# Down projections as seven block products, with block sums made during the gate stages

## The chip, the cores and the metric

The kernel runs on one core of one Trainium2 chip. The metric is the device time of one execution in microseconds; the figure for a kernel is the median of its runs. The time before is 2503.31 us (three runs, 2498.36 to 2503.79).

## The reference

Two decoder layers over 1024 tokens of width 1024, in float32. Layer 0 uses sliding-window attention, layer 1 stick-breaking attention; each attention and each channel mixer is normalised, scaled by the conditioning vector `c`, and added to the residual through a gate. What the change touches is the channel mixer:

```python
D_FF = 2816
def swiglu(h, w_gate, w_up, w_down):
    return (jax.nn.silu(h @ w_gate) * (h @ w_up)) @ w_down
...
    for i in range(DEPTH):
        mod = (cond @ ada_w[i] + ada_b[i])[:, None, :]
        sh1, sc1, g1, sh2, sc2, g2 = jnp.split(mod, 6, axis=-1)
        ...
        h = rmsnorm(x, norm2_g[i]) * (1.0 + sc2) + sh2
        x = x + g2 * swiglu(h, w_gate[i], w_up[i], w_down[i])
```

`c` is (1, 1024), `x` is (1, 1024, 1024), `w_gate` and `w_up` are (2, 1024, 2816), `w_down` is (2, 2816, 1024).

## The kernel before, in words

The program runs through these stages, with their place in the profiled span in microseconds: norm and attention of layer 0 (to about 335), its output projection with the second norm (335 to 452), the gates of layer 0 (452 to 905), down of layer 0 (907 to 1148), attention of layer 1, its output projection, the gates of layer 1 (1850 to 2249), down of layer 1 (2251 to 2493).

Every product is done in three matmuls. An operand is split into a rounded high part and a remainder (ScalarE casts, VectorE subtracts: `split_s` with L629/L630 in the gates, `split_into` with L308/L309 elsewhere), and `mm3` (L108) multiplies high by high, low by high and high by low, each 128x128 by 128x512.

**Gates** (`gates`, L816). 22 feature tiles are taken two at a time, so there are 11 chunks. A chunk splits the 1024 tokens in two halves and its weights in 2x2 blocks, and makes for the gate matrix and for the up matrix seven block products instead of eight (`first_product` with B11, then B21, T2, T3, N4, T1, B22): 14 products of 12 matmuls, 168 in all. The block sums of the weights are made by GpSimd (`block_sums`, L804 to L806, and L812), 8 operations a chunk. Sums of products are read from PSUM by VectorE (L814, L840, L848, L851, L855, L858). Two PSUM banks of tag `z` hold T2, T3 and N4 in turn: the sum u2 (L814) has to be read before T3 may add to the same bank, and u3 (L848) before N4 may. At the end SiLU (ScalarE) and a multiply (L862) make four quarters of the hidden tile, which go to DRAM (`hid`, stores at L841 and L863).

In layer 0 the gates also carry the conditioning products of layer 1. `ada_step` (L262) loads 512 KB tiles into the pool `ad`, which has two buffers, and VectorE multiplies and accumulates them (L268); every eighth such step ends in 8 small matmuls. `grow_make` borrows the same pool once.

**Down** (`down`, L873). The hidden tiles and the rows of `w_down` are loaded again, 44 tiles of 512 KB a layer. The weight tile is multiplied by the gate row g2 (L889), both are split (L308, L309), and 22 x 8 x 2 x 3 = 1056 matmuls a layer run in six rounds of up to four feature tiles. Each bank is added to the accumulator `xacc` by VectorE (`evict`, L906), 96 times a layer. `xacc` is loaded at the start from `xsp` (`load_acc`, L941), and stored by block at the end.

**Order.** Each engine works through its own list in a fixed order, and so does the queue of SyncE that issues nearly all DMAs: an instruction that waits holds back all that stand behind it in its list. The build makes these lists from the program text, its priorities and the reuse of buffers; they aren't the order of the text. `rows(range(4, 8))` in `out_proj` (L671, L672 on GpSimd) belongs to the norm between output projection and gates.

Of the kernel before, what the change touches and what calls it, by code (L numbers as in the profile page):

```python
# [64 lines left out]
def build(tc, x_in, c_in, pos_in, ada_w, ada_b, n1g, n2g, wqkv_a, qn_a, kn_a, sinks, wo_a,  # L65
# [750 lines left out]
    def gates(l, H, p, fp, hid, ada_per, first):  # L816
# [10 lines left out]
        def chunk(c):  # L827
            if c == 0:
                m = first["m"]
            else:  # L830
# [10 lines left out]
            nc.sync.dma_start(hid[2 * c][:, 0:512], g11)  # L841
# [17 lines left out]
            for n, i, j in (("p1", 1, 0), ("u3", 1, 1), ("u2", 0, 1)):  # L859
# [16 lines left out]

    def down(l, rawp, nraw, dn, xacc, hid, row, finish):
        f0 = 0
        for r, n in enumerate(ROUNDS):
            g = r % 2  # L880
            T = []
            for j in range(n):
                f = f0 + j
                t = []
                for e, src in enumerate((hid[f], w_down[l][f * P : (f + 1) * P])):
                    raw = rawp.tile([P, D], F32, tag="raw", name=nm("raw"), bufs=nraw)
                    ld = nc.sync.dma_start(raw, src)
                    if e:
                        nc.vector.tensor_tensor(raw, raw, row, op=ALU.mult)  # L889
                    h = dn.tile([P, D], F32R, tag=f"{'ab'[e]}h{g}{j}", name=nm("dh"), bufs=1)  # L890
                    l_ = dn.tile([P, D], F32R, tag=f"{'ab'[e]}l{g}{j}", name=nm("dl"), bufs=1)
                    t += split_into(h, l_, raw)
                T.append(t)
            f0 += n
            if r == 0:
                with tc.issue_after(ld.ins):
                    load_acc(xacc)

            def one(pb, b, h, j):
                ah, al, bh, bl = T[j]  # L900
                mm3(pb, ah[:, b * P : (b + 1) * P], al[:, b * P : (b + 1) * P],
                    bh[:, h * 512 : (h + 1) * 512], bl[:, h * 512 : (h + 1) * 512], j == 0, j == n - 1)

            def evict(pb, b, h):
                xs = xacc[b][:, h * 512 : (h + 1) * 512]
                nc.vector.tensor_tensor(xs, pb, xs, op=ALU.add)  # L906

            if r == 0:
                pbs = [bank(t) for t in BANKS]
                for j in range(n):  # L910
                    for i in range(8):
                        one(pbs[i], i // 2, i % 2, j)
                for i in range(8):
                    evict(pbs[i], i // 2, i % 2)
            for b in range(4 if r == 0 else 0, NB):
                for h in range(2):
                    pb = bank(BANKS[(2 * b + h) % 8])
                    for j in range(n):
                        one(pb, b, h, j)
                    evict(pb, b, h)  # L920
                if r == len(ROUNDS) - 1:
                    finish(b)

    def mixer(l, W, p, od, x_src, gi, ada_per, rest, row):
# [308 lines left out]
```

## Time and profile before

| | before |
|---|---|
| median of three runs, us | 2503.31 |
| profiled execution, us | 2499.7 |
| its span, us | 2497.6 |
| mean granted clock of TensorE | 0.978 |
| TensorE matmuls, busy us (share of span) | 2355.8 (94%) |
| VectorE, busy us | 1615.5 (65%) |
| ScalarE, busy us | 1034.4 (41%) |
| GpSimd, busy us | 641.1 (26%) |
| moved by DMA, MB | 273.78 |

The span is what the trace covers; 2.1 us of the profiled execution's time lie around it. In the rows PE is TensorE, DVE VectorE, ACT ScalarE, POOL GpSimd and SP SyncE. The granted clock is a share of full speed. A busy engine isn't necessarily the one that the others wait for; that is read from a stage at a time.

### The profile page before, as it was taken

The page shows a single profiled execution, that of the slowest core. Times are in us where ns is not written, and L with a number is a line of the kernel's source. Part 1 is how long each engine was busy: PE and PEld are TensorE (multiplying, and loading weights), DVE is VectorE, ACT ScalarE, POOL GpSimd, SP SyncE. Part 2 cuts the span into 40 slices and gives each one's busy share as a digit, 9 for nine tenths or more (in the row PEclk, how much of TensorE's full clock was granted, in tenths as well). Part 3 has the DMA queues.
Part 4 walks back from the last instruction along what each step waited for, and adds up shares of the span by engine and source line. Part 5 has one row for each costly group of instructions (what it writes and reads, how often), then busy time and mean ns, then how long its engine had stood idle before and what let it go on. Part 6 is the DMA issues. An engine that isn't in the chain of part 4 may idle for free.

```text
span 2497.6 us, 31454 instructions
## 1 busy us (share of the span) xinstructions
PE 2355.8 (94%) x11404; PEld 1933.1 (77%) x11404; DVE 1615.5 (65%) x2335; ACT 1034.4 (41%) x2029; POOL 641.1 (26%) x671
## 2 busy tenths in 40 slices
PE   6799799799999999999999999989979999999999
PEld 6677577578787878887788888877758888887887
DVE  7678967765767566637666666696475554558553
ACT  4477733423232322104666666673343333323110
POOL 2443522223232300001444444441222322310000
PEclk9799999899999999999999999999989999999999
DMA  8113488234545363302222222127512232227211
GB/s 289 51 37 117 132 229 239 61 114 124 176 119 175 98 236 127 126 1 93 74 60 59 56 56 59 50 83 166 166 54 73 84 93 64 93 89 259 83 51 68
DMA packets 187196, 273.78 MB, mean 110 GB/s; under 512 B 11793, under 2 KB 131745, under 8 KB 187041
## 3 DMA queue, kind: packets, MB, share of 16 engines
q1 hardware_dynamic: 186416, 271.63, 35.7%
q8 instruction: 90, 1.47, 0.3%
q14 instruction: 66, 0.53, 0.1%
q10 hardware_dynamic: 624, 0.14, 0.0%
HBM read 206.72 MB, written 56.62 MB: 105 GB/s over the span
## 4 chain that ended last, share of the span: by engine, by line
PE 74%; DVE 12%; DMA 5%; ACT 3%; POOL 3%; issue 2%; ACTq 0%; SPq 0%; DVEq 0%; POOLq 0%
PE psz L108 25%; PE psd L108 23%; PE pst L108 17%; PE psa L108 6%; DMA ada<-in_ada_w_dram 3%; PE pst L116 3%; DVE nb L1102 2%; DVE acc L268 2%; DVE al L119 1%; ACT sm L534 1%; DVE lT L119 1%; DVE sl L630 1%; DVE Wl L309 1%; ACT nb L1095 0%; ACT bb L1096 0%
## 5 line engine op out<-in xcount | busy, mean ns | idle before, releaser
L629 ACT CAST sh<-rg 128x512 fp32r<-128x512 f32 x308 | 191.5, 622 | 568.7 <-PE psz L108 249.9
L108 PE MATMUL psd<-hth,whl 128*128 128x512 f32 x768 | 302.3, 412 | 0.1
L630 DVE TENSOR_TENSOR sl<-rg,sh 128x512 fp32r<-128x512 f32 x308 | 237.1, 770 | 82.0 <-ACT sh L629 81.9
L1104 POOL TENSOR_TENSOR bb<-bb,nb 128x895 f32<-128x895 f32 (+7 forms) x128 | 171.5, 1342 | 243.8 <-DVE nb L1102 149.5
L1102 DVE TENSOR_TENSOR_SCAN nb<-nb,ones 128x896 f32<-128x896 f32 (+7 forms) x128 | 194.4, 1521 | 45.2 <-ACT nb L1095 44.8
L308 ACT CAST dh<-raw 128x1024 fp32r<-128x1024 f32 x88 | 88.0, 1049 | 277.6 <-PE psa L108 175.4
L804 POOL TENSOR_TENSOR rg<-rg,rg 128x512 f32<-128x512 f32 x44 | 62.0, 1408 | 511.4 <-DMA rg<-in_w_up_dram 333.6
L108 PEld LDWEIGHTS psd<-hth,whl 128*128 128x128 f32 x768 | 145.2, 189 | 21.5 <-issue 0.7
L108 PE MATMUL psz<-hT,sh 128*128 128x512 f32 x352 | 139.9, 401 | 18.9 <-ACT hT L685 10.0
L108 PE MATMUL psd<-htl,whl 128*128 128x512 f32 x384 | 151.5, 397 | 1.7 <-DVE htl L119 1.6
L119 DVE TENSOR_TENSOR al<-pst,ah 128x512 fp32r<-128x512 f32 x160 | 108.4, 684 | 60.8 <-ACT ah L1125 57.7
L108 PE MATMUL psz<-lT,sh 128*128 128x512 f32 x352 | 139.6, 397 | 2.4 <-DVE lT L119 2.4
L108 PE MATMUL psz<-hT,sl 128*128 128x512 f32 x352 | 138.7, 394 | 0.0
L108 PE MATMUL psd<-hB,sh 128*128 128x512 f32 x352 | 138.1, 392 | 0.0
L108 PE MATMUL psd<-hB,sl 128*128 128x512 f32 x352 | 137.6, 391 | 0.0
L108 PE MATMUL psd<-lB,sh 128*128 128x512 f32 x352 | 137.5, 391 | 0.0
L268 DVE SCALAR_TENSOR_TENSOR acc<-ada,condT,acc 128x1024 f32<-128x1024 f32 x77 | 108.2, 1405 | 35.4 <-DMA ada<-in_ada_w_dram 34.7
L1095 ACT ACTIVATE nb<-psz 128x448 f32<-128x448 f32 (+3 forms) x192 | 95.6, 498 | 60.2 <-PE psz L108 56.8
L1125 ACT CAST ah<-pst 128x512 fp32r<-128x512 f32 x160 | 94.2, 594 | 47.8 <-PE pst L116 45.5
L309 DVE TENSOR_TENSOR dl<-raw,dh 128x1024 fp32r<-128x1024 f32 x88 | 104.5, 1218 | 9.2 <-ACT dh L308 9.1
L108 PE MATMUL psz<-QK,QK 128*128 128x384 f32 (+4 forms) x384 | 105.2, 355 | 1.7 <-ACT bb L1096 1.7
L108 PE MATMUL psz<-dl,dh 128*128 128x512 f32 x264 | 103.2, 391 | 0.0
(325 smaller groups left out, 6346.0 us busy)
## 6 DMA issues: line engine op xcount, KB each, us to landing
ada<-in_ada_w_dram SPq DMA_DIRECT2D x96, 512.0 KB, 5.3
rg<-in_w_gate_dram SPq DMA_DIRECT2D x44, 512.0 KB, 3.9
rg<-in_w_up_dram SPq DMA_DIRECT2D x44, 512.0 KB, 5.0
raw<-hid SPq DMA_DIRECT2D x44, 512.0 KB, 6.9
raw<-in_w_down_dram SPq DMA_DIRECT2D x44, 512.0 KB, 4.6
hid<-f SPq DMA_DIRECT2D x64, 256.0 KB, 2.1
wr<-in_wqkv_b_dram SPq DMA_DIRECT2D x24, 512.0 KB, 4.1
odA<-ob SPq DMA_DIRECT2D x32, 256.0 KB, 2.5
```

Source lines behind the costliest of these rows:

```text
L108: chained(nc.tensor.matmul(o, l, r, start=start, stop=stop, skip_group_check=more))
L116: chained(nc.tensor.transpose(o, i, ident[:n, :n]))
L119: return nc.vector.tensor_tensor(o, a, h.bitcast(F32), op=ALU.subtract)
L268: i = nc.vector.scalar_tensor_tensor(a, wt, condT[:, j : j + 1], a, op0=ALU.mult, op1=ALU.add)
L308: nc.scalar.copy(h, raw)
L309: (eng or nc.vector).tensor_tensor(l, raw, h.bitcast(F32), op=ALU.subtract)
L629: nc.scalar.copy(hv, src)
L630: nc.vector.tensor_tensor(lv, src, hv.bitcast(F32), op=ALU.subtract)
L1095: nc.scalar.activation(nb[:, s0 : s0 + e], pz[:, 0:e], AF.Sigmoid, scale=-1.0)
L1102: nc.vector.tensor_tensor_scan(rv, rv, ones[:, 0:1].to_broadcast([P, L]), initial=1.0, op0=ALU.mult, op1=ALU.mult)
L1104: nc.gpsimd.tensor_tensor(bb[:, 0 : L - 1], bb[:, 0 : L - 1], nb[:, 1:L], op=ALU.mult)
L1125: nc.scalar.copy(ah_, pt)
```

## The change

Down is done by 2x2 blocks too. The tokens are halved, the 1024 output columns are halved, and the feature tiles are taken as even and odd ones. Seven products over all 11 pairs of feature tiles take the place of eight: numbers 1 to 7 in the code, made in the order 1, 6, 2, 7, 5, 4, 3. Each has 4 token blocks x 11 x 3 = 132 matmuls, 924 a layer. They run in two groups of four PSUM banks, X and Y; 6 and 7 share Y, 1 and 2 share X, and a group is read by VectorE when a product ends. The gate row is applied when a bank is read (`rows_of`) and no longer to the weights. The last product runs bank by bank.

The products need sums of blocks of both operands. Sums of the hidden blocks (S1 to S4) are made at the end of a gates chunk by GpSimd, four operations (L867, L871, L873, L875), and 7 tiles of 256 KB a chunk go to DRAM instead of 4 (`store`, L829). Sums of `w_down` are made in the gates too: `down_sums` (L900) loads two tiles of 512 KB a chunk into the pool `ad` (L907), does four subtractions on GpSimd (L910), and stores two tiles of 512 KB to DRAM (`wT`, L915 and L916). Down then loads 7 x 11 x 2 half tiles of 256 KB, mostly two in one DMA: 84 loads a layer (L923).

```diff
-    def gates(l, H, p, fp, hid, ada_per, first):
+    def gates(l, H, p, fp, ada_per, first):
...
+            def store(n, t):
+                nc.sync.dma_start(hidS[n, c // 2][:, c % 2], t)
+
+            down_sums(l, c)
...
             tt(g11, m[1]["X"], g11, op=ALU.mult)
-            nc.sync.dma_start(hid[2 * c][:, 0:512], g11)
...
                 tt(g, m[1][n], g, op=ALU.mult)
-                nc.sync.dma_start(hid[2 * c + i][:, j * 512 : j * 512 + 512], g)
+                if n == "p1":
+                    pt_(g11, g11, g, op=ALU.add)
+                    store("S1", g11)
+                store({"p1": "A22", "u3": "A12", "u2": "A11"}[n], g)
+            s2, s3, s4 = (m[1][n] for n in ("u2", "p1", "u3"))
+            pt_(s2, g11, m[0]["u2"], op=ALU.subtract)
+            store("S2", s2)
+            pt_(s4, m[0]["u3"], s2, op=ALU.subtract)
+            store("S4", s4)
+            pt_(s3, m[0]["p1"], s2, op=ALU.subtract)
+            store("S3", s3)
...
-    def down(l, rawp, nraw, dn, xacc, hid, row, finish):
...
+    ND = 26
+    LHS = {1: "A11", 2: "A12", 3: "S4", 4: "A22", 5: "S1", 6: "S2", 7: "S3"}
+    STEPS = [(2 * t, min(2, NC - 2 * t)) for t in range((NC + 1) // 2)]
...
+    def down_sums(l, c):
+        R = []
+        for i in range(2):
+            r = ad.tile([P, D], F32, tag="ad", name=nm("dw"), bufs=2)
+            nc.sync.dma_start(r, w_down[l][(2 * c + i) * P : (2 * c + i + 1) * P])
+            R += [r[:, 0:512], r[:, 512:D], r]
+        b11, b12, r0, b21, b22, r1 = R
+        sb = lambda o, a, b: nc.gpsimd.tensor_tensor(o, a, b, op=ALU.subtract)
+        sb(b11, b12, b11)
+        sb(b12, b22, b12)
+        sb(b22, b22, b11)
+        sb(b21, b21, b22)
+        nc.sync.dma_start(wT[0, c // 2][:, c % 2], r0)
+        nc.sync.dma_start(wT[1, c // 2][:, c % 2], r1)
+
+    def down(l, rawp, nraw, dn, xacc, row, finish):
+        tt = nc.vector.tensor_tensor
+        def load(src, n, which):
+            raw = rawp.tile([P, 2, 512], F32, tag="raw", name=nm("raw"), bufs=nraw)
+            ld = nc.sync.dma_start(raw[:, 0:n], src)
+            h, l_ = (dn.tile([P, 2, 512], F32R, tag="dn", name=nm("d" + which + e), bufs=ND) for e in "hl")
+            split_into(h[:, 0:n], l_[:, 0:n], raw[:, 0:n])
+            return h, l_, ld
...
+        product(1, X, True)
+        t1 = []
+        for i in range(4):
+            t = rawp.tile([P, 2, 512], F32, tag="t1", name=nm("t1"), bufs=4)
+            for h in range(2):
+                rows_of(X[i], h, t[:, h])
+            t1.append(t)
+        product(6, Y, True)
+        product(2, X, False)
...
+        product(3, X, False, True)
+        for i in range(4):
+            add(rows_of(Y[i], 0), i, 0)
+            finish(i)
+        for i in range(4):
+            add(rows_of(X[i], 1), 4 + i, 1)
+            finish(4 + i)
```

The lists of the engines change at three places that the prediction speaks of.

**The queue of SyncE in the gates of layer 0, from chunk 4 to chunk 5.** `ada` are the conditioning loads, `dw` the loads of `w_down` for the sums, `rg` loads of gate and up weights; `hidA` and `hidS` are stores of blocks and sums. Before:

```order
L863 DMA hid_3760<-p_1148_5888 128x512
L783 DMA rg_6464<-in_w_up_dram 128x4x256
L863 DMA hid_3760<-f_6007 128x512
L262 DMA ada_6448<-in_ada_w_dram 128x1024
L262 DMA ada_6451<-in_ada_w_dram 128x1024
L863 DMA hid_3759<-f_5951 128x512
L262 DMA ada_6454<-in_ada_w_dram 128x1024
```

Now:

```order
L829 DMA hidA_3759<-f_6116 128x512
L907 DMA dw_6287<-in_w_down_dram 128x1024
L829 DMA hidA_3753<-f_6060 128x512
L829 DMA hidS_3783<-f_6080 128x512
L829 DMA hidS_3765<-f_6134 128x512
L829 DMA hidS_3789<-p_1162_6017 128x512
L915 DMA wT_3795<-dw_6285 128x1024
L916 DMA wT_3801<-dw_6287 128x1024
L262 DMA ada_6579<-in_ada_w_dram 128x1024
L262 DMA ada_6582<-in_ada_w_dram 128x1024
L262 DMA ada_6585<-in_ada_w_dram 128x1024
```

The conditioning loads stand behind three more hidden stores and two stores of weight sums; all of them use the two buffers of `ad`. What runs on GpSimd from the A11 multiply to the second weight store, now:

```order
L871 TENSOR_TENSOR f_6080<-f_6057,f_6060 128x512
L873 TENSOR_TENSOR f_6134<-f_6116,f_6080 128x512
L875 TENSOR_TENSOR p_1162_6017<-p_1158_5998,f_6080 128x512
L910 TENSOR_TENSOR dw_6285<-dw_6287,dw_6285 128x512
L806 TENSOR_TENSOR rg_6301<-rg_6301,rg_6299 128x4x128
L910 TENSOR_TENSOR dw_6287<-dw_6287,dw_6285 128x512
L910 TENSOR_TENSOR dw_6287<-dw_6287 128x512
```

Seven operations stand in a row, where one (the L806) stood. VectorE at the same place, now:

```order
L844 TENSOR_TENSOR f_6379<-psd_6322,f_6379 128x512
L630 TENSOR_TENSOR sl_6423<-rg_6295,sh_6422 128x512
L268 SCALAR_TENSOR_TENSOR acc_6283<-ada_6579,condT,acc_6283 128x1024
L268 SCALAR_TENSOR_TENSOR acc_6283<-ada_6582,condT,acc_6283 128x1024
L814 TENSOR_TENSOR f_6382<-psz_6383,p_1213_6320 128x512
```

Two accumulations, whose tiles are loaded behind the weight stores, stand ahead of the u2 sum (L814), which T3 waits for.

**GpSimd at the end of the output projection of layer 0.** L671 and L672 are the norm of one token block. Before:

```order
L671 TENSOR_SCALAR ss_4510<-ss_4510 128x1
L672 TENSOR_TENSOR ss_4510<-ss_4510,mhalf 128x1
L812 TENSOR_TENSOR rg_4420<-rg_4422,rg_4420 128x4x128
L671 TENSOR_SCALAR ss_4516<-ss_4516 128x1
L672 TENSOR_TENSOR ss_4516<-ss_4516,mhalf 128x1
```

Now:

```order
L812 TENSOR_TENSOR rg_4452<-rg_4454,rg_4452 128x4x128
L910 TENSOR_TENSOR dw_5001<-dw_5001 128x512
L910 TENSOR_TENSOR dw_5001<-dw_5003,dw_5001 128x512
L910 TENSOR_TENSOR dw_5003<-dw_5003,dw_5001 128x512
L910 TENSOR_TENSOR dw_5003<-dw_5003 128x512
L671 TENSOR_SCALAR ss_4542<-ss_4542 128x1
L672 TENSOR_TENSOR ss_4542<-ss_4542,mhalf 128x1
```

The four weight sums of chunk 1 stand ahead of the norm of the last four token blocks.

**The queue of SyncE between the gates and down of layer 0.** Before:

```order
L863 DMA hid_3772<-p_1460_7692 128x512
L863 DMA hid_3772<-f_7811 128x512
L863 DMA hid_3771<-f_7755 128x512
L887 DMA raw_8031<-in_w_down_dram 128x1024
L887 DMA raw_8038<-hid_3754 128x1024
```

Now:

```order
L829 DMA hidA_3756<-f_7966 128x512
L829 DMA hidS_3786<-f_7986 128x512
L829 DMA hidS_3768<-f_8040 128x512
L829 DMA hidS_3792<-p_1486_7923 128x512
L923 DMA raw_8226<-in_w_down_dram 128x2x512
L923 DMA raw_8232<-hidA_3751 128x1024
```

Before, five tile loads of down stand ahead of the last three hidden stores; now the first load stands behind all seven stores of chunk 10, the three sums among them. In layer 1 five loads stand ahead of the last stores.

## Rows read from the trace of the kernel before

**Rows 1.** The page: busy time, share and count of TensorE and GpSimd.

```profile
PE 2355.8 (94%) x11404; PEld 1933.1 (77%) x11404; DVE 1615.5 (65%) x2335; ACT 1034.4 (41%) x2029; POOL 641.1 (26%) x671
```

**Rows 2.** Windows: gates 0, down 0, gates 1 (columns in the first line).

```profile
core 0: us, PE busy (x) PEld busy (x) DVE busy (x) ACT busy (x) POOL busy (x), PEclk, DMA share, GB/s
620.00:660.00 40.00, 38.63 (x175) 31.23 (x174) 30.90 (x36) 11.66 (x20) 11.04 (x8) 1.00 0.61 184
...
925.00:1190.00 265.00, 261.35 (x1174) 213.93 (x1173) 158.62 (x203) 65.55 (x80) 9.31 (x17) 1.00 0.29 95
...
1880.00:2220.00 340.00, 339.95 (x1496) 280.38 (x1496) 176.77 (x249) 108.69 (x181) 99.11 (x70) 1.00 0.26 80
```

**Rows 3.** The chain of waits: start, length, what (matmuls back to back in down).

```profile
932.32 2.72 PE psd L108 x12
```

**Rows 4.** Groups by line: operation, tile, count | busy us, mean ns | idle before, releaser.

```profile
L308 ACT CAST dh<-raw 128x1024 fp32r<-128x1024 f32 x88 | 88.0, 1049 | 277.6 <-PE psa L108 175.4
...
L309 DVE TENSOR_TENSOR dl<-raw,dh 128x1024 fp32r<-128x1024 f32 x88 | 104.5, 1218 | 9.2 <-ACT dh L308 9.1
```

**Rows 5.** One line's instructions, ns min/median/max: the bank sum of down, and the split subtract.

```profile
L906 DVE TENSOR_TENSOR xa<-psz,xa x72: 680/691/692, 928.3 to 2491.8; 128x512 f32<-128x512 f32 x72
...
L630 DVE TENSOR_TENSOR sl<-rg,sh x308: 673/683/1806, 399.8 to 2242.0; 128x512 fp32r<-128x512 f32 x154
```

**Rows 6.** DMA issues: KB each, median us from issue to landing.

```profile
ada<-in_ada_w_dram SPq DMA_DIRECT2D x96, 512.0 KB, 5.3
...
raw<-in_w_down_dram SPq DMA_DIRECT2D x44, 512.0 KB, 4.6
...
xsp<-xa SPq DMA_DIRECT2D x8, 512.0 KB, 2.6
```

**Rows 7.** The chain of waits: two places of gates 0, one of gates 1.

```profile
496.98 10.88 PE psd L108 x48
...
633.95 4.26 DMA ada<-in_ada_w_dram
...
638.31 1.29 DVE acc L268
...
1982.96 10.88 PE psd L108 x48
1993.85 16.32 PE psz L108 x72
```

**Rows 8.** Timeline: VectorE and GpSimd, chunk 3 of gates 0 and one of gates 1.

```profile
625.32 1.29 POOL L806 TENSOR_TENSOR rg<-rg,rg 128x512 f32<-128x512 f32 x1 [1.83 <-DVE sl L630]
625.39 2.30 DVE L268 SCALAR_TENSOR_TENSOR acc<-ada,condT,acc 128x1024 f32<-128x1024 f32 x1 [0.21 <-DMA ada<-in_ada_w_dram]
...
635.05 1.27 DVE L268 SCALAR_TENSOR_TENSOR acc<-ada,condT,acc 128x1024 f32<-128x1024 f32 x1
...
1984.21 0.68 DVE L862 TENSOR_TENSOR f<-f,f 128x512 f32<-128x512 f32 x1
```

**Rows 9.** Timeline: GpSimd and TensorE at the end of output projection 0.

```profile
441.49 0.86 POOL L672 TENSOR_TENSOR ss<-ss,mhalf 128x1 f32<-128x1 f32 x1
...
452.47 0.53 PE L108 MATMUL psz<-hT,sh 128*128 128x512 f32 x1 [3.61 <-ACT hT L685]
```

**Rows 10.** Timeline: from gates to down, layer 0 and layer 1.

```profile
907.03 0.32 SPq L863 DMA_DIRECT2D hid<-f  x1
907.37 0.51 PE L108 MATMUL psd<-dh,dh 128*128 128x512 f32 x1 [1.89 <-ACT dh L308]
...
2251.42 0.65 PE L108 MATMUL psd<-dh,dh 128*128 128x512 f32 x1 [1.90 <-ACT dh L308]
```

**Rows 11.** Windows around an idle TensorE, and the chain piece behind the first of them.

```profile
909.00:914.00 5.00, 4.67 (x14) 3.69 (x14) 4.82 (x5) 2.00 (x2) 0.00 (x0) 0.66 0.86 266
914.00:920.00 6.00, 6.00 (x28) 4.96 (x27) 3.55 (x4) 3.05 (x3) 0.00 (x0) 1.00 1.02 406
...
478.43 8.12 PE psz L108 x24
```

More of the change, by code (lines that the diff above doesn't have):

```diff
@@ L871, in gates @@
         return row
-    ROUNDS = (4, 4, 4, 4, 4, 2)
     BANKS = ["d", "z", "t", "d", "z", "t", "z", "a"]
-    def down(l, rawp, nraw, dn, xacc, hid, row, finish):
[L878 to L922, printed above, removed]
@@ new lines, in down, with operands, one, product @@
+    def down(l, rawp, nraw, dn, xacc, row, finish):
[6 more added lines that the diff above has]
+            return h, l_, ld
+        def operands(q, t):
+            n = STEPS[t][1]
+            bh, bl, _ = load(rhs(l, q, t), n, "b")
+            ah, al, ld = load(hidS[LHS[q], t][:, 0:n], n, "a")
+            return ah, al, bh, bl, ld
+        def one(pb, i, T, e, start, stop):
+            ah, al, bh, bl, _ = T
+            s = slice(i * P, (i + 1) * P)
+            mm3(pb, ah[:, e, s], al[:, e, s], bh[:, e], bl[:, e], start, stop, True)
+        def product(q, pbs, start, by_bank=False):
+            last = len(STEPS) - 1
+            if by_bank:
+                Ts = [operands(q, t) for t in range(len(STEPS))]
+                for i in range(4):
+                    for t, T in enumerate(Ts):
+                        for e in range(STEPS[t][1]):
+                            one(pbs[i], i, T, e, start and t == 0 and e == 0, t == last)
+                return
+            for t in range(len(STEPS)):
+                T = operands(q, t)
+                if q == 1 and t == 2:
+                    with tc.issue_after(T[4].ins):
+                        load_acc(xacc)
+                for e in range(STEPS[t][1]):
+                    for i in range(4):
+                        one(pbs[i], i, T, e, start and t == 0 and e == 0, t == last)
+        def rows_of(pb, h, t=None):
+            t = t or rawp.tile([P, 512], F32, tag="tm", name=nm("tm"), bufs=2)
+            tt(t, pb, row[:, h * 512 : (h + 1) * 512], op=ALU.mult)
+            return t
+        def add(t, b, h):
+            xs = xacc[b][:, h * 512 : (h + 1) * 512]
+            tt(xs, xs, t, op=ALU.add)
+        X = [bank(t) for t in BANKS[:4]]
+        Y = [bank(t) for t in BANKS[4:]]
+        product(1, X, True)
[7 more added lines that the diff above has]
+        product(2, X, False)
+        for i in range(4):
+            add(t1[i][:, 1], 4 + i, 1)
+            add(t1[i][:, 0], i, 0)
+            add(t1[i][:, 1], i, 1)
+        for i in range(4):
+            add(rows_of(Y[i], 1), 4 + i, 1)
+        product(7, Y, False)
+        for i in range(4):
+            add(rows_of(X[i], 0), 4 + i, 0)
+        X = [bank(t) for t in BANKS[:4]]
+        product(5, X, True)
+        for i in range(4):
+            add(rows_of(Y[i], 1), i, 1)
+        product(4, Y, False)
+        for i in range(4):
+            add(rows_of(X[i], 1), i, 1)
+        product(3, X, False, True)
+        for i in range(4):
+            add(rows_of(Y[i], 0), i, 0)
+            finish(i)
+        for i in range(4):
+            add(rows_of(X[i], 1), 4 + i, 1)
+            finish(4 + i)
@@ L929, in mixer @@
         cm_fp, fp = pools.open(f"fp{l}", "left")
-        row2 = gates(l, H, p, fp, hid, ada_per, first)
+        row2 = gates(l, H, p, fp, ada_per, first)
         rest()
@@ L964, in build @@
     xacc = [xq.tile([P, D], F32, tag="xq", name=nm("xa"), bufs=NQ) for _ in range(NB)]
-    down(0, rw, 5, dn, xacc, hid, row2, lambda b: nc.sync.dma_start(xsp[b], xacc[b]))
+    down(0, rw, 5, dn, xacc, row2, lambda b: nc.sync.dma_start(xsp[b], xacc[b]))
     pools.close(cm_rw)
```

12 lines of the change are left out of this document (10 added, 2 removed).

## Prediction

> **What bounds the kernel now.** I read the page first: TensorE is busy for 94% of the span and GpSimd for 26% [rows 1]. An average doesn't say which stage waits for what, so the windows by stage come next [rows 2]. In down of layer 0 TensorE is busy for 261.35 of 265 us at full granted clock, VectorE for 158.62: the matmuls are the bound. In the gates of layer 1 they are so without a gap, 339.95 of 340. In the gates of layer 0 a 40 us stretch with many conditioning loads has 38.63 us of TensorE and 30.90 of VectorE. There the chain of waits leaves TensorE and runs through a conditioning load (4.26 us) and its accumulation on VectorE (1.29) [rows 7]. So layer 0's gates already stand at the edge of a second bound, the one that this change loads.
>
> **Matmuls removed.** 1056 - 924 = 132 a layer, 264 in all. The chain of waits has 12 of them in 2.72 us [rows 3], 0.2267 each, and down has no other bound: **-59.8 us**. Down then has 924 x 0.2267 = 209.5 us of matmuls a layer, if its cover holds. VectorE: 154 half tiles are 77 full ones, 77 x 1.218 = 94 [rows 4], and 68 reads and adds of banks at 0.69 make 47 [rows 5]; 141 of 209.5, and the row multiplies are gone. ScalarE: 77 x 1.05 = 81 [rows 4]. DMA: 154 x 256 KB are 40 MB, with the accumulator in and out 49 MB, 233 GB/s; the trace shows 406 at the start of down [rows 11]. So nothing is added here.
>
> **Gates of layer 0.** A chunk gets 8 more GpSimd operations, two loads and two stores of 512 KB, and three more hidden stores. The new wait is a ring: `ad` has two buffers, and a conditioning load may only overwrite one when the sum in it has been stored. I walk it for chunk 5, with T for the chunk's first matmul. In gates 1 T is 1982.96, and T3 starts 5.44 us into the `psz` piece of 1993.85, at T + 16.3 [rows 7]. The A11 multiply of the chunk before ends at 1984.89, T + 1.9 [rows 8]. By the new list GpSimd then has the L806 due there and seven operations, 8 x 1.29 = 10.3 [rows 8], to T + 12.2. The second weight store takes 2.6 [rows 6], the load behind it 4.3 [rows 7], the accumulation 1.27 [rows 8], the u2 sum 0.69 [rows 5]: T + 21.0. T3 was due at T + 16.3, so TensorE waits 4.7 us.
>
> The same walk over each chunk's list, with its own loads and accumulations, gives about 1, 4.3, 2.7, 3.3, 4.7, 0, 4.0, 4.4, 1 and 3 for chunks 1 to 10: 28 us. About 10 come off, since the old waits (1.37 of 40 us idle in the stretch above [rows 2]) lie in the same places: 18. Then the clock. After an idle TensorE, 24 matmuls took 8.12 us where two pieces of 12 take 5.44 [rows 3, 11]; after the short waits at the start of down the granted clock was 0.66 over 5 us, 1.7 us lost [rows 11]. Six waits of over 2.5 us, at 1.6 each, add 9. For splits and sums that meet a GpSimd operation on the way I add 3. Sum **+30**. Bounds: +5, if loads and stores run so far ahead that only the old waits remain; +58, if VectorE can't keep up (the first rival).
>
> **Norm of layer 0.** Four weight sums of 1.29 stand ahead of the norm of the last four token blocks. In the trace that norm's last step ends at 442.35, and TensorE then idles 3.61 us before 452.47 [rows 9]: it is on the path. **+5**; 0 if the norm comes later than its list position allows, +10 if the weight tiles come late (another 4.6 [rows 6]).
>
> **From gates to down, layer 0.** Now TensorE restarts at 907.37 [rows 10], since its first tiles are long there. With the change the first load waits in the queue behind the S3 store. The A11 store goes out at 907.03 [rows 10]; three sums bring 910.9; the load lands 4.6 us later [rows 6], and two casts of 1.05 end at 917.6, some 0.4 later with issue times. That is 10.6 us late, and the longer idle costs more clock than the 1.7 of now: **+11**, between +8 (landing in 2.6, the least in [rows 6]) and +15.
>
> **Gates of layer 1.** No conditioning loads there, so the ring has only weight tiles, loaded early. GpSimd goes from 8 to 16 operations a chunk, 20.6 of 38 us. At three chunk boundaries four to eight weight sums stand in a block before an operation that the next split needs; 14 splits in 38 us come every 2.7, and three buffers leave a split one such step and a little in hand. **+4**, between 0 and +12. **From gates to down, layer 1, and the end:** five loads stand ahead of the last stores, so TensorE restarts about as now [rows 10] and waits once for the sixth, 1.5 us; one weight sum is ahead of the norm (0.8); the last bank takes a multiply and an add, not one add, 0.7 [rows 5]. **+3**, 0 to +6.
>
> **Sum.** -59.8 + 30 + 5 + 11 + 4 + 3 = -6.8. Against the profiled execution, 2499.7, this gives 2492.9; the median of the runs lies 3.6 above that execution, so 2496.5 by it. I take 2495.
>
> **Rival 1, slower: VectorE and GpSimd hold each other up.** An accumulation took 2.30 us where it began beside a GpSimd operation of 1.29, and 1.27 where none ran [rows 8]: the VectorE operation took as long as if it had waited for the other to end. In a chunk of gates 0 GpSimd will have 16 x 1.29 = 20.6 us; VectorE has 14 splits of 0.68 [rows 5], 3 multiplies of 0.68 [rows 8] and five accumulations of 1.27, 18 us, that read two tiles of SBUF, and 11 sums from PSUM at 0.69, 7.6. If VectorE stands still for all of GpSimd's time, a chunk takes 46.2 us. It takes 40.85 now: from 496.98 to the last product at 905.48, ten chunks [rows 7, 10]. That is +54 in place of +30, a sum of +17, **2521**. It decides once a chunk exceeds 40.85 + 3.7 = 44.5, where the other terms leave nothing over. Against it: the sums from PSUM can pass beside GpSimd, and VectorE has 9 us of 40 to spare [rows 2]. The Trainium skill states such a rule (SBUF — State Buffer, "Who interferes with whom"): VectorE with two SBUF inputs and a GpSimd operation that reads SBUF exclude each other, and the later one blocks fully. The 2.30 us agree with it [rows 8]; it speaks against this change, and by it the price lies nearer to this rival's.
>
> **Rival 2, clearly faster.** The stores and loads of a chunk run in time that the old list left empty, and the waits replace the old ones rather than add to them: gates 0 at +8. -59.8 + 8 + 5 + 11 + 4 + 3 = -29, **2474**. For it: DMA is used to 0.61 in the busiest stretch of the gates [rows 2]. Against it: the walk is made of steps in a row, not of bandwidth.
>
> **Rival 3, down bound by its loads.** A raw buffer is held for landing, cast and subtract, 4.6 + 1.05 + 1.22 = 6.9 us [rows 4, 6]; five buffers give a load every 1.4 us, 84 loads 116 us. With landings of 10 us it would be 2.45 a load, 206 us, as long as the matmuls, with waits of some 12 a layer, -6.8 + 24 = +17: **2519**. The kernel moves half the bytes per us in this stage that the trace shows at its start, so this is unlikely.
>
> **How the numbers follow.** Forecast 0.50 (2481 to 2511), rival 1 0.22, rival 2 0.22, rival 3 0.06. A measurement of this kernel can tell some 0.2%, about 5 us, from no change. The forecast's half, spread evenly, has 0.29 below 2498, 0.17 within 5 us of 2503.3 and 0.04 above. With rival 2 faster has 0.51, same 0.17, and with rivals 1 and 3 slower has 0.32. All low ends together give -47, all high ends +41; the range is 2464 to 2526, from the middle of rival 2's further side to just past rival 1. The likeliest case's own range is 2481 to 2511.
>
> **What would show it.** In the profile after: both downs about 30 us shorter with TensorE busy throughout (else rival 3); an idle of some 10 us before down in layer 0 and none such in layer 1; in gates 0 TensorE idle before T3 and N4, ended by a u2 or u3 sum behind an accumulation, with the granted clock at half after it; the norm of the last four blocks 5 us later. If chunks of gates 0 take 44 us I am right, at 46 rival 1 is, at 41.6 rival 2. Accumulations and split subtracts that mostly take far longer than 1.27 and 0.68 us would speak for rival 1 as the cause. Wrong would be the whole if down doesn't shorten.

## The result and the profile after

The changed kernel takes **2545.51 us** (median of four runs, 2544.27 to 2548.24), the kernel before 2503.55 beside it: ratio 1.0172 [1.0153, 1.0190], 42 us slower. The forecast was 2495, and the range ended at 2526. In the profiled executions the span grew from 2497.6 to 2543.6 us, by 46.0.

The page after, first line, answers to [rows 1]; then one window a stage (gates 0, down 0, gates 1, down 1), in the columns of [rows 2]:

```profile
PE 2326.9 (91%) x11140; PEld 1903.1 (75%) x11140; DVE 1642.7 (65%) x2315; ACT 1106.1 (43%) x2109; POOL 898.9 (35%) x847
```

```profile
core 0: us, PE busy (x) PEld busy (x) DVE busy (x) ACT busy (x) POOL busy (x), PEclk, DMA share, GB/s
498.00:961.00 463.00, 418.01 (x1797) 337.85 (x1795) 286.34 (x344) 119.82 (x200) 226.52 (x152) 0.95 0.53 173
974.00:1186.00 212.00, 211.96 (x924) 174.48 (x923) 129.74 (x149) 82.55 (x90) 0.00 (x0) 0.99 0.63 218
1918.00:2305.00 387.00, 370.51 (x1604) 303.62 (x1604) 208.96 (x265) 114.93 (x191) 202.22 (x144) 0.98 0.41 132
2330.00:2541.00 211.00, 208.53 (x918) 172.27 (x916) 128.01 (x149) 74.69 (x79) 0.00 (x0) 1.00 0.63 214
```

TensorE has 264 matmuls fewer, yet its busy time fell by 28.9 us only, since many ran at a lower granted clock (0.960 in the mean, 0.978 before). Down 0 has no gap: 211.96 of 212 us. The gates show the loss: in gates 0 TensorE stands still for 45 of 463 us, where in the same stage before it was busy for 400.48 of 409:

```profile
core 0: us, PE busy (x) PEld busy (x) DVE busy (x) ACT busy (x) POOL busy (x), PEclk, DMA share, GB/s
497.00:906.00 409.00, 400.48 (x1796) 326.13 (x1795) 270.78 (x346) 121.07 (x201) 113.89 (x76) 1.00 0.45 137
```

By the starts and ends of the stages' matmuls, in us:

| | before | after | change | forecast |
|---|---|---|---|---|
| up to chunk 1 of gates 0 | 496.8 | 497.9 | +1.0 | +5 |
| gates 0, chunks 1 to 10 | 408.7 | 463.0 | +54.3 | +30 |
| idle before down 0 | 1.9 | 12.7 | +10.8 | +11 |
| down 0 | 242.6 | 212.7 | -29.9 | -29.9 |
| attention, output projection, norm of layer 1 | 716.5 | 727.8 | +11.3 | +0.8 |
| gates 1, chunks 1 to 10 | 383.1 | 405.6 | +22.5 | +4 |
| idle before down 1 | 1.9 | 7.1 | +5.2 | +1.5 |
| down 1 | 241.7 | 211.9 | -29.8 | -29.9 |
| end | | | +0.6 | +0.7 |

**Gates 0, chunk 5**, which the prediction walked through. Timelines of GpSimd, SyncE's queue, VectorE and TensorE (start, duration, what, and in brackets the idle time before it and what ended it), with one line of what the queue waited for (behind the colon: us in total, times, longest); the chunk's first matmul starts at T = 684.46:

```profile
687.66 1.29 POOL L871 TENSOR_TENSOR f<-f,f 128x512 f32<-128x512 f32 x1
690.61 1.81 POOL L875 TENSOR_TENSOR p<-p,f 128x512 f32<-128x512 f32 x1
693.64 1.74 POOL L806 TENSOR_TENSOR rg<-rg,rg 128x512 f32<-128x512 f32 x1
696.70 1.28 POOL L910 TENSOR_TENSOR dw<-dw 128x512 f32<-128x512 f32 x1
...
698.01 0.32 SPq L916 DMA_DIRECT2D wT<-dw  x1
698.42 8.59 SPq L262 DMA_DIRECT2D ada<-in_ada_w_dram  x4
...
SPq L262 <- DMA wT<-dw: 2.5, 1, 2.5
...
702.74 1.28 DVE L268 SCALAR_TENSOR_TENSOR acc<-ada,condT,acc 128x1024 f32<-128x1024 f32 x1 [1.71 <-DMA ada<-in_ada_w_dram]
705.36 1.28 DVE L268 SCALAR_TENSOR_TENSOR acc<-ada,condT,acc 128x1024 f32<-128x1024 f32 x1 [1.34 <-DMA ada<-in_ada_w_dram]
706.57 0.68 DVE L814 TENSOR_TENSOR f<-psz,p 128x512 f32<-128x512 f32 x1
...
707.40 0.77 PE L108 MATMUL psz<-hT,sh 128*128 128x512 f32 x1 [6.44 <-DVE f L814]
```

The chain is the one forecast: a row of GpSimd sums, the second weight store, the conditioning load that waits for its landing, accumulation, u2, T3. GpSimd ends at T + 13.5, not T + 12.2, since some of its operations take 1.6 to 1.8 us. The store takes 3.3 us to land (698.01 to 701.31), not 2.6; the load behind it and its one accumulation, the second of the two shown, take about what was forecast. TensorE waits 6.44 us, not 4.7.

**Gates 1, chunk 4.** Its first matmul starts at 2031.96. The chain of waits here:

```profile
2030.93 7.17 DMA rg<-in_w_gate_dram
...
2039.50 2.50 POOL rg L805 x2
...
2046.13 1.29 POOL dw L910
2047.42 1.25 POOL f L871
2048.67 1.25 POOL dw L910
...
2052.37 1.22 POOL rg L806
2053.59 1.22 POOL dw L910
2054.81 1.23 POOL rg L812
...
2056.06 0.63 ACT sh L629
```

The queue of SyncE shows why the gate weights came at that time:

```profile
2027.00 0.33 SPq L915 DMA_DIRECT2D wT<-dw  x1
2027.38 0.43 SPq L783 DMA_DIRECT2D rg<-in_w_up_dram  x1
2030.07 0.33 SPq L916 DMA_DIRECT2D wT<-dw  x1
2030.45 1.46 SPq L783 DMA_DIRECT2D rg<-in_w_gate_dram  x2
```

The load stands behind two stores that wait for GpSimd's weight sums. So GpSimd begins the block sums of the gate weights (L804) 6.3 us after the chunk's first matmul, where it began them 4.7 us ahead of it in the kernel before (there the first matmul of that chunk starts at 2020.88). Before, then after:

```profile
2016.17 1.29 POOL L804 TENSOR_TENSOR rg<-rg,rg 128x512 f32<-128x512 f32 x1 [4.90 <-DMA rg<-in_w_gate_dram]
...
2038.25 1.29 POOL L804 TENSOR_TENSOR rg<-rg,rg 128x512 f32<-128x512 f32 x1 [3.30 <-DMA rg<-in_w_gate_dram]
```

Then the other sums of its blocks (L805, L806, L812) stand in GpSimd's list among seven sums, four of weights and three hidden ones, that nothing in this chunk needs. TensorE waits 8.13 us at 2058.55, and 5.59 at 2105.40 in the next chunk; the other chunks with 8 more GpSimd operations take 38.1 to 40.2 us, as before.

### The profile page after: what moved, and what is told of

It reads as the page before. It is cut to its first block, busy times and chain, and to the rows that moved or that the text cites. A ratio compares the mean times of both kernels' runs of the same rounds, so it can differ in the third digit from the quotient of the medians.

```text
span 2543.6 us, 31733 instructions
## 1 busy us (share of the span) xinstructions
PE 2326.9 (91%) x11140; PEld 1903.1 (75%) x11140; DVE 1642.7 (65%) x2315; ACT 1106.1 (43%) x2109; POOL 898.9 (35%) x847
## 3 DMA queue, kind: packets, MB, share of 16 engines
q1 hardware_dynamic: 229072, 369.69, 46.2%
## 5 line engine op out<-in xcount | busy, mean ns | idle before, releaser
L630 DVE TENSOR_TENSOR sl<-rg,sh 128x512 fp32r<-128x512 f32 x308 | 289.5, 942 | 130.1 <-ACT sh L629 125.2
L108 PE MATMUL psz<-hT,sh 128*128 128x512 f32 x352 | 146.9, 420 | 50.5 <-DVE f L814 24.8
L804 POOL TENSOR_TENSOR rg<-rg,rg 128x512 f32<-128x512 f32 x44 | 60.7, 1380 | 340.5 <-DMA rg<-in_w_up_dram 262.3
L308 ACT CAST dah<-raw 128x1024 fp32r<-128x1024 f32 x84 | 82.5, 982 | 165.5 <-PE psa L108 77.2
L108 PE MATMUL psz<-lT,sh 128*128 128x512 f32 x352 | 146.1, 415 | 1.9 <-DVE lT L119 1.8
L108 PE MATMUL psz<-hT,sl 128*128 128x512 f32 x352 | 144.6, 411 | 1.2 <-DVE sl L630 1.2
L309 DVE TENSOR_TENSOR dal<-raw,dah 128x1024 fp32r<-128x1024 f32 x84 | 95.2, 1133 | 70.4 <-ACT dah L308 69.4
L268 DVE SCALAR_TENSOR_TENSOR acc<-ada,condT,acc 128x1024 f32<-128x1024 f32 x77 | 106.5, 1384 | 49.1 <-DMA ada<-in_ada_w_dram 48.5
L108 PEld LDWEIGHTS psz<-hT,sh 128*128 128x128 f32 x352 | 70.3, 201 | 74.9 <-issue 27.1
L309 DVE TENSOR_TENSOR dbl<-raw,dbh 128x1024 fp32r<-128x1024 f32 x84 | 95.0, 1131 | 44.4 <-ACT dbh L308 43.7
```

The costliest lines, as they stand in the source:

```text
L108: chained(nc.tensor.matmul(o, l, r, start=start, stop=stop, skip_group_check=more))
L268: i = nc.vector.scalar_tensor_tensor(a, wt, condT[:, j : j + 1], a, op0=ALU.mult, op1=ALU.add)
L308: nc.scalar.copy(h, raw)
L309: (eng or nc.vector).tensor_tensor(l, raw, h.bitcast(F32), op=ALU.subtract)
L630: nc.vector.tensor_tensor(lv, src, hv.bitcast(F32), op=ALU.subtract)
L804: nc.gpsimd.tensor_tensor(A[1, 0], A[1, 0], A[1, 1], op=ALU.add)
```

## Experiments

A time without an interval is that of one run, beside a run or runs of the kernel before on the same chip; those took 2494.45 to 2507.99 us. Gates 0 and gates 1 mean chunks 1 to 10, as in the table; after has 463.0 and 405.6, before 408.7 and 383.1. Five runs with the old gates of layer 0 took 406.0 to 409.9 us there, so a difference of 4 us in gates 0 says nothing.

**1. Which of the added work costs?** The weight sums left out altogether (down reads blocks of `w_down` in their place, the same bytes), and then only the four subtractions left out, with all their loads and stores kept:

```diff
-            down_sums(l, c)
```
```diff
-        sb(b11, b12, b11)
-        sb(b12, b22, b12)
-        sb(b22, b22, b11)
-        sb(b21, b21, b22)
```

> The weight sums leave the gates: down_sums isn't called, and down reads plain halves of w_down where it read sums, as many bytes in the same shapes (this leaves the weight sums out of the computation). The changed kernel's gates stages took 462.9 us (layer 0, chunk 1 to the end) and 405.6 us (layer 1), the kernel before 408.5 and 382.9. Theory A (GpSimd operations hold up VectorE, each of the eight new ones a chunk alike): the four hidden sums stay, so about half of the loss stays: gates 0 about 436, gates 1 about 394, time about 2505. Theory B (the two-buffer ring and the queue order: conditioning loads and gate loads wait behind weight stores, which wait for sums, which wait for loads): the loss goes, gates 0 at 405 to 415, gates 1 at 383, time 2455 to 2470.

> The weight tiles are loaded into the ring and stored to DRAM in the gates as in the change, but GpSimd makes no sums of them (this leaves the weight sums out of the computation). Theory A: as the run without weight sums, about 2505 with gates 0 about 436. Theory B: the ring and the queue stay, shortened by some 5 us a chunk of sums in the walk: gates 0 at 430 to 455, gates 1 at 385 to 400, time 2485 to 2525.

Measured: 2484.70 us without weight sums (gates 433.0 and 383.6), 2484.71 with their traffic alone (428.6 and 383.7); before 2494.45. By themselves the traffic and the ring of two buffers cost nothing: GpSimd's subtractions, with the stores that wait for them, cost 30 to 34 us in gates 0 and all of the 22 in gates 1. The hidden sums, with their stores, cost the other 24 of gates 0 (433.0 - 408.7).

**2. More sums without traffic.** On the kernel without weight sums, S2 and S4 are made twice and S3 three times:

```diff
             pt_(s2, g11, m[0]["u2"], op=ALU.subtract)
+            pt_(s2, g11, m[0]["u2"], op=ALU.subtract)
...
+            for _ in range(3):
+                pt_(s3, m[0]["p1"], s2, op=ALU.subtract)
```

> As the run without weight sums (their part is left out of the computation in the same way), but S2 and S4 are made twice and S3 three times, so that GpSimd has as many operations a chunk as in the changed kernel (16), with no loads, stores or ring behind the four added ones. Theory A: gates 0 near 460 and gates 1 near 405 again, time about 2535. Theory B: as the run without weight sums, within 10 us.

Measured: 2571.43 us, gates 479.6 and 411.5. Four operations a chunk at this place cost 46.6 and 27.9 us, more than the weight sums with their traffic. They add no traffic, but the three hidden stores come later by them too.

**3. SyncE's queue.** Without weight sums, the stores of S2, S4 and S3 in layer 0 are held back until behind the conditioning loads of the next chunk:

```diff
-            store("S2", s2)
+            late.append(("S2", s2, store))
...
+                with tc.issue_after(ada_ld[0].ins):
+                    for n, t, st_ in late[:-3]:
+                        st_(n, t)
```

> As the run without weight sums (they are left out of the computation again; gates 0 took 433.0 us there against 408.7 before, with four hidden sums a chunk on GpSimd), but in layer 0 the stores of S2, S4 and S3 are held back until a chunk later, behind conditioning loads that stood behind them. GpSimd has the same work. Theory B1 (the queue of SyncE: a store that waits for GpSimd's sums holds back the conditioning loads): gates 0 at 408 to 417. Theory A (GpSimd's operations hold up VectorE's): gates 0 stays at 428 to 436.

Measured: 2476.84 us, gates 424.8 and 383.5. So about 8 of the hidden sums' 24.3 us (433.0 - 424.8, one run each) were conditioning loads behind a store that waited for a sum. What is left stands in the timeline of this run, first VectorE, then GpSimd (lines count one up here: L269 is the accumulation, L631 the split, L807 and L813 the block sums):

```profile
626.82 1.78 DVE L631 TENSOR_TENSOR sl<-rg,sh 128x512 fp32r<-128x512 f32 x1
628.52 2.31 DVE L269 SCALAR_TENSOR_TENSOR acc<-ada,condT,acc 128x1024 f32<-128x1024 f32 x1
630.75 3.47 DVE L631 TENSOR_TENSOR sl<-rg,sh 128x512 fp32r<-128x512 f32 x2
634.15 4.54 DVE L269 SCALAR_TENSOR_TENSOR acc<-ada,condT,acc 128x1024 f32<-128x1024 f32 x2
639.22 0.68 DVE L631 TENSOR_TENSOR sl<-rg,sh 128x512 fp32r<-128x512 f32 x1
...
625.77 2.27 POOL L871 TENSOR_TENSOR f<-f,f 128x512 f32<-128x512 f32 x1
628.13 1.62 POOL L873 TENSOR_TENSOR f<-f,f 128x512 f32<-128x512 f32 x1
629.71 2.27 POOL L875 TENSOR_TENSOR p<-p,f 128x512 f32<-128x512 f32 x1
631.94 1.74 POOL L807 TENSOR_TENSOR rg<-rg,rg 128x512 f32<-128x512 f32 x1
633.64 3.98 POOL L813 TENSOR_TENSOR rg<-rg,rg 128x512 f32<-128x512 f32 x2
```

For 11 us neither engine is idle, and both are slow: splits 1.7 us in place of 0.68, accumulations 2.3 in place of 1.27, GpSimd up to 2.27 in place of 1.29. They look like taking turns. Once GpSimd is done, at 637.6, splits have their short duration again.

**4. Turns, list or tile?** Three kernels without weight sums put work that nothing needs at the idle place of GpSimd's list, behind the last L812: four subtractions that read p1; nine memsets, which read nothing; four subtractions of a tile of their own.

```diff
+            z = tile_()
+            for _ in range(4):
+                pt_(z, m[0]["p1"], m[0]["p1"], op=ALU.subtract)
```
```diff
+            for _ in range(9):
+                nc.gpsimd.memset(z, 0.0)
```
```diff
+            nc.gpsimd.memset(z, 0.0)
+            z2 = tile_()
+            for _ in range(4):
+                pt_(z2, z, z, op=ALU.subtract)
```

> As the run without weight sums, with four more GpSimd operations of 128x512 a chunk whose result nobody reads, placed where GpSimd's list was idle (ahead of the next chunk's first weight sum, behind this chunk's last). No store waits for them. GpSimd is as loaded as in the changed kernel, 16 operations a chunk. Theory A: gates 0 near 455 to 463 again, gates 1 at 390 to 405. Theory B1: gates 0 at 430 to 438, gates 1 at 383 to 386: what counts is who waits for an operation, not how many there are.

> The same kernel as the one with four dead GpSimd sums a chunk, but the four sums, which read tiles of SBUF, are nine memsets of one tile at the same place of the list, which read nothing and keep GpSimd busy for about as long. Theory A, GpSimd and VectorE exclude each other when both read SBUF, and the four sums cost because VectorE stands still for them: the memsets cost VectorE nothing, gates 0 is near the 433 us of the run without weight sums and gates 1 near 383.6, a time near 2486. Theory B, the list: what stands behind four more operations of GpSimd comes later, whatever they read: gates 0 near 445 and gates 1 near 397 as with the dead sums, a time near 2513. Between them: some of each.

> Four dead GpSimd subtractions a chunk at the place of the nine memsets of the run before, behind the last L812 of a chunk, but of a tile of their own that nothing else writes or reads: they read SBUF as the four dead sums of the first such run did, and hold no tile that the chunk needs. Theory A, exclusion: VectorE stands still for them, gates 0 near 445 us and gates 1 near 397, as with the dead sums that read p1. Theory B: those cost because SiLU of p1 had to wait until they had read it, a wait that this kernel doesn't have: gates 0 near 433 and gates 1 near 383.6, as with the memsets.

| at the idle place | us | gates 0 | gates 1 |
|---|---|---|---|
| nothing | 2484.70 | 433.0 | 383.6 |
| 9 memsets | 2480.66 | 433.4 | 383.7 |
| 4 subtractions, own tile | 2493.33 | 440.1 | 383.5 |
| 4 subtractions of p1 | 2513.15 | 445.2 | 397.2 |

The 13.6 us of the subtractions of p1 in gates 1 come neither from turns nor from the list, since the same four on another tile, at the same place, cost nothing there: SiLU works in place on p1's tile and had to wait until the dead sums had read it. The trace names it (ScalarE, groups of gates 1: busy, mean ns, idle before and its releasers):

```profile
L866 ACT ACTIVATE p<-p 128x512 f32<-128x512 f32 x10 | 6.3, 632 | 37.2 <-POOL f L856 36.6 <-DVE p L863 0.6
```

Between memsets and subtractions of an own tile only the reading of SBUF differs much, and the times differ by 6.7 us in gates 0 and by nothing in gates 1. VectorE's groups of gates 0, with the memsets and then with the subtractions:

```profile
L630 DVE TENSOR_TENSOR sl<-rg,sh 128x512 fp32r<-128x512 f32 x138 | 131.6, 958 | 17.6 <-ACT sh L629 17.5
L268 DVE SCALAR_TENSOR_TENSOR acc<-ada,condT,acc 128x1024 f32<-128x1024 f32 x42 | 61.1, 1454 | 26.5 <-DMA ada<-in_ada_w_dram 26.0
```
```profile
L630 DVE TENSOR_TENSOR sl<-rg,sh 128x512 fp32r<-128x512 f32 x138 | 137.3, 999 | 18.0 <-ACT sh L629 15.6 <-POOL rg L806 2.4
L268 DVE SCALAR_TENSOR_TENSOR acc<-ada,condT,acc 128x1024 f32<-128x1024 f32 x42 | 68.7, 1636 | 23.3 <-DMA ada<-in_ada_w_dram 22.9
```

The same 180 VectorE operations take 13.3 us longer (5.7 + 7.6). With nothing at the place the means were 960 and 1433, but 973 and 1593 in the run of experiment 3, so these two runs alone don't settle it. The trace with the memsets does, within one run: VectorE, then GpSimd, in gates 0.

```profile
672.52 2.31 DVE L268 SCALAR_TENSOR_TENSOR acc<-ada,condT,acc 128x1024 f32<-128x1024 f32 x1
680.71 2.60 DVE L268 SCALAR_TENSOR_TENSOR acc<-ada,condT,acc 128x1024 f32<-128x1024 f32 x2 [2.48 <-DMA ada<-in_ada_w_dram]
...
672.13 1.62 POOL L875 TENSOR_TENSOR f<-f,f 128x512 f32<-128x512 f32 x1
673.71 2.27 POOL L877 TENSOR_TENSOR p<-p,f 128x512 f32<-128x512 f32 x1
680.57 5.19 POOL L856 MEMSET f<- 128x512 f32 x9
```

Beside two sums an accumulation takes 2.31 us, beside memsets two take 2.60. Over chunks 1 to 10 of both layers, accumulations took 1.28 us in the mean with nothing on GpSimd beside them (17) and with memsets alone (11), and 1.80 with a sum or subtraction (14); splits took 0.68 (105), 0.68 (35) and 1.14 (136). So VectorE does stand still for GpSimd operations that read SBUF, and not for memsets.

**5. The same at the busy place**, among the hidden sums and ahead of the block sums: nine memsets of S4's tile, or four subtractions of that tile by itself, which also leave zeros.

```diff
             pt_(s4, m[0]["u3"], s2, op=ALU.subtract)
+            for _ in range(9):
+                nc.gpsimd.memset(s4, 0.0)
```
```diff
+            for _ in range(4):
+                pt_(s4, s4, s4, op=ALU.subtract)
```

> The hidden sums without the weight sums, and nine memsets of one tile a chunk (4.7 us of GpSimd, by 0.527 us each) among the hidden sums, ahead of the L806 and the L812 that are due there; the run with four more subtractions at this place had 479.6 and 411.5 us of gates, the one without them 433.0 and 383.6. The sum S4 is overwritten by zeros. Theory A, exclusion: memsets read nothing, so gates 0 near 433 to 440 and gates 1 near 384 to 388. Theory B, the list: L806 and L812 come 4.7 us later whatever stands ahead of them: gates 0 near 475 and gates 1 near 408.

> The run with nine memsets of S4's tile at the busy place, but four subtractions of that tile by itself in their place: one of them ahead of the second L806, three ahead of the first L812 (the memsets: one and five). They keep GpSimd busy for 5.2 us by 1.3 each, the memsets for 4.7, and read SBUF, which the memsets don't. With memsets the gates took 443.0 and 383.6 us. Theory A, exclusion adds to the list order: gates 0 clearly longer, by the 7 us or more that reading cost at the idle place, near 450 to 460; gates 1 up to 398. Theory B, the list alone: within 2 or 3 us of 443.0, and 383.6.

Measured: 2505.72 us with the memsets (gates 443.0 and 383.6), 2556.64 with the subtractions (475.4 and 398.1). Standing ahead in the list costs 10 us in gates 0 and nothing in gates 1; subtractions in place of memsets add 32 and 14.5. In gates 0 that isn't reading alone: with the memsets two conditioning loads stand ahead of S4's store in SyncE's queue, with the subtractions one. In gates 1 there are no such loads, and nine of the ten chunks wait 1.22 us for a split behind an L812.

**6. Other places for the work.** The stores of S2 to S4 and of the weight sums issued by GpSimd; the weight sums of layer 1 made during down 0; and the old gates and old down kept in layer 0, with layer 1 alone on seven products and its weight sums made in down 0.

```diff
-            store("S2", s2)
+            store("S2", s2, nc.gpsimd)
...
-        nc.sync.dma_start(wT[0, c // 2][:, c % 2], r0)
+        nc.gpsimd.dma_start(wT[0, c // 2][:, c % 2], r0)
```
```diff
-            down_sums(l, c)
+            if l == 0:
+                down_sums(l, c)
...
+                    with tc.issue_after(T[4].ins):
+                        down_sums(1, (steps[0] - 6) // 3)
```
```diff
-    down(0, rw, 5, dn, xacc, row2, lambda b: nc.sync.dma_start(xsp[b], xacc[b]))
+    down_old(0, rw, 5, dn, xacc, hid, row2, lambda b: nc.sync.dma_start(xsp[b], xacc[b]))
...
+                with tc.issue_after(ld.ins):
+                    down_sums(1, c_)
```

> The change as it is, but GpSimd's queue issues the stores of S2, S3, S4 and of the weight sums, so that SyncE's queue waits for none of them. A conditioning load still waits for its buffer in the ring. Theory A alone: gates 0 at 460 to 470, gates 1 at 403 to 410, time about 2545. Theory B1 as the larger part: gates 0 at 435 to 448 (from 463), gates 1 at 385 to 395 (from 405.6), the idle ahead of down 0 at 5 to 9 us instead of 12.7; time 2500 to 2520. Each DMA that GpSimd issues costs it some time, which would show as longer idles before its sums.

> The weight sums of layer 1 are made in down of layer 0, with sums of their own in DRAM for each layer and each chunk's loads issued behind a load of down. Both theories: gates 1 at 383 to 384 from 405.6, the norm before it back by 6 us. Down 0 gets 44 GpSimd sums and 23 MB of traffic: theory A 215 to 225 us (VectorE, 142 of 213 us, is held up), B1 213. Time 2512 to 2525 (A) or 2508 to 2518 (B1) against 2545.

> The change in layer 1 alone: layer 0 keeps its gates and its down as before and makes layer 1's weight sums in down 0, where GpSimd is idle; layer 1 gets hidden sums and the seven products. Both theories: gates 0 at 409, gates 1 at 383 to 385 (hidden sums alone cost nothing there), down 1 at 212 instead of 242, some 5 us more idle ahead of it. Down 0 at 243, by theory A up to 255, as VectorE is held up by 57 us of sums. Time about 2503 - 30 + 5 = 2478 on the chip of the first runs, 25 below the kernel before; with theory A at its worst 2490.

Measured: GpSimd's queue made it worse, 2574.23 us, gates 474.9 and 413.9. Sums in down 0: 2545.95, no gain; gates 1 fell to 383.5, but down 0 rose from 212.7 to 245.9. A first version, in which layer 1's weight sums overwrote those of layer 0, took 2549.13. The waits of SyncE's queue in the second version (behind the colon: us in total, times, longest): its weight stores stand for 126 us waiting for the sums, and down's own loads behind them.

```profile
SPq L916 <- POOL dw L911: 63.2, 20, 4.6
SPq L917 <- POOL dw L911: 63.0, 20, 4.3
```

Layer 1 alone: 2486.52 us, and in a second set of four runs 2484.73 (ratio to before 0.9948 [0.9931, 0.9964]); gates 406.0 and 383.5, down 0 256.4 and then 250.1. That is 12 us faster than before.

**7. The last version twice more**, with the loads and stores of the weight sums issued by GpSimd, and then also with the first loads of the next stage (`wr`) put behind down's last load:

```diff
-            nc.sync.dma_start(r, w_down[l][(2 * c + i) * P : (2 * c + i + 1) * P])
+            nc.gpsimd.dma_start(r, w_down[l][(2 * c + i) * P : (2 * c + i + 1) * P])
```
```diff
+            with tc.issue_after(last_ld[-1].ins):
+                nc.sync.dma_start(raw, src)
```

> As the run with the change in layer 1 alone (2486.5 us beside 2497.1 before; its down 0 took 256.4 us, not 243, since VectorE and ScalarE waited for loads of down that stood behind stores of sums), but GpSimd's own queue issues the loads of weight tiles and the stores of their sums in down 0, so that nothing on SyncE's queue waits for a sum. Theory B1 (queue order): down 0 at 243 to 246 us, time 2474 to 2479 beside 2497. Theory A (GpSimd's operations hold up VectorE's): the split subtracts keep their 1.46 us mean and down 0 stays at 252 to 257, time about 2486.

> As the run with GpSimd's own queue (2520.0 us beside 2500.7), but layer 1's first attention weight loads, which share the two-buffer ring with the weight sums and stood in SyncE's queue ahead of 8 loads of down, are issued behind down's last load. In that run SyncE waited 51.0 us for the ring there, and TensorE idled 38.98 us in one piece. Theory C (in-order waits alone: the ring and the list position made that idle): down 0 goes from 286.6 to 243 to 248 us, time 2475 to 2482 beside 2500.7. Theory A (GpSimd's sums hold up VectorE): the mean of down's subtracts stays at 1.40 us instead of 1.22, and down 0 stays over 250 us.

Measured: 2519.97 us (1.0080 [1.0063, 1.0097]) and **2477.71 us** (0.9919 [0.9904, 0.9933]). In the first a load `wr`, which uses the `ad` ring too, waited 72 us for that ring (51.0 for a load of a weight tile, then 21.3 for a store of sums) with eight of down's loads behind it in SyncE's queue, and TensorE idled 38.98 us ahead of 1062.27. The second takes that away; its down 0 has 246.7 us, gates 409.9 and 383.5. It is the fastest of all, 19 us ahead of before: layer 1's saving of 29.4 (241.7 to 212.3), less 5.5 of idle before down 1 and 4.1 in down 0.

## Why the prediction was wrong

- **Matmuls: right.** -59.8 forecast, -59.7 measured, and the cover held: down's loads land in a median of 4.4 to 5.3 us, and 218 GB/s were enough. Rival 3 is out.
- **Gates 0: the walk was right in kind and half in size.** It gave waits of 1, 4.3, 2.7, 3.3, 4.7, 0, 4.0, 4.4, 1 and 3 us for chunks 1 to 10; the trace has 0.4, 6.1, 4.1, 6.6, 6.4, 1.2, 6.3, 7.9, 0 and 5.7. That is 45 for 28, in the chunks that were named. The old waits take 8.5 off, so **+36 in place of +18**. The **clock term** was 9, for six waits at 1.6 each, though its own list has seven of over 2.5 us, as the trace has; TensorE's busy time grew by 17.5, 2.5 for each of seven, at a mean granted clock of 0.95. The step that failed is "the same walk over each chunk's list, with its own loads and accumulations": it took each operation at the duration that it has alone, 1.29, 1.27 or 0.68 us, with 3 us added for meetings in the whole stage, though [rows 8] had the 2.30. By the windows above GpSimd's operations in this stage took 1.49 us each (226.52 / 152), and 1.50 before (113.89 / 76); the walk's eight come to 12.0 us by that, not 10.3. Chunk 5 shows where its 1.7 us went; of the other chunks only the waits are known, not each step.
- **Rival 1 had the price** of gates 0, +54: chunks take 46.3 us in the mean (463.0 / 10), where it gave 46.2. That they agree so well is luck: its sum leaves VectorE no idle time, and VectorE was busy for 286 of the 463 us. Its total was lower, 2521, for want of the terms below. Its mechanism is real, by the memsets of experiment 4 and in the changed kernel itself: in chunks 1 to 10 of both layers 160 splits with a GpSimd operation beside them took 1.14 us in the mean, the other 116 took 0.68; accumulations 1.79 (12) and 1.28 (30). This agrees with what the Trainium skill says (SBUF — State Buffer, "Who interferes with whom") of VectorE with two SBUF inputs and a GpSimd operation that reads SBUF. But it is not the whole: about 8 us of the hidden sums' cost were SyncE's queue, and being ahead in the list cost 10 at the busy place. Rival 2, +8 in gates 0, is out. The median split still took 692 ns, not far more than 0.68, which the prediction had set as the mark of this rival; the mean, 942 for 770, is what moved. Accumulations took no longer in the mean than before, 1384 ns for 1405.
- **Gates 1: +22.5 for +4.** The prediction priced the block of sums ahead of an L806 and said of the ring that it "has only weight tiles, loaded early". The failed step is the second: the ring's stores wait for the sums, and gate loads stand behind them in SyncE's queue. In chunk 4 GpSimd then begins the block sums 11 us later against the chunk's start, and meets the seven other sums in its list, 9 us of them. Two chunks take 13 and 8 us longer than the others (51.4 and 45.7, 38.1). Without the subtractions, with the same traffic, the stage is back at 383.7.
- **Norm of layer 0: +1.0 for +5**, near the lower bound of 0. **Idle before down 0: +10.8 for +11**, by the steps given: last A11 store at 962.43, sums, first load at 966.81, first cast at 970.86.
- **Layer 1 before the gates: +11.3 for 0.8.** All but one weight sum was left out of the price. 5.1 us come right behind down 0, 4.45 of them in one wait, where a memset of attention waits for down's last matmul and holds the norm of the first token blocks in GpSimd's list:

```profile
1186.29 0.20 POOL L1178 MEMSET bb<- 128x128 f32 x1 [219.92 <-PE psd L108]
1186.58 0.22 POOL L1072 TENSOR_SCALAR ss<-ss 128x1 f32<-128x1 f32 x1
...
1190.67 0.33 PE L116 MATMUL psa<-ident,xa 128*128 128x128 f32 x1 [4.45 <-DVE xa L1074]
```

The other 6.2 are in output projection and norm 1, with the weight sums ahead of the norm. Without weight sums the whole stretch takes 721.3 us, 6.5 less.
- **Idle before down 1: +5.2 for +1.5.** The cast waits 6.35 us for the last A11 tile, which is stored at the end of the gates and loaded again.

All the high ends of the prediction's own terms add up to +41, and +42 was measured; its range stopped at 2526, short of that sum.

What stays open is the division of gates 0's 54 us between turns and list order. The two kernels of experiment 5 differ in the queue's order as well as in reading, and no run takes the turns away from the changed kernel itself.

## What to carry to other kernels

Work that is given to an engine with much idle time is not free: ask what stands behind it in that engine's list, which stores wait for it and what stands behind those in the DMA queue, and whether the two vector engines then read SBUF at the same time. Price such walks with the durations that operations have when another engine is at work, not with the shortest ones. And a saving can be kept while its cost is avoided: here the layer without conditioning loads takes the seven products and makes its weight sums in a stage that has room for them.

## What the runs showed that was not expected

Nine GpSimd memsets a chunk, 4.7 us, cost nothing that shows at the idle place and 10 us at the busy one, while four subtractions of about that length cost 6.7 and up to 42. A DMA issued by GpSimd took 0.55 to 0.58 us of that engine (22 loads, 12.2 us; 22 stores, 12.6, in the runs of experiment 7). Stores moved there stand between the sums in that engine's list, which may be why it made the changed kernel slower; no run shows that by itself. And a dead operation can cost more by the tile that it reads than by its time: 13.6 us in gates 1, where the same four operations on another tile cost nothing.
